# MLP up products by Strassen's scheme: seven block products instead of eight

## The chip, the cores and the metric

The kernel runs on one core of a Trainium2 chip. The metric is the device time of one execution in microseconds (us); the kernel before has a median of 1849.1 us over three runs (1847.06 to 1849.63).

## What is computed

Three layers of width D = 1024 on S = 512 tokens: gated linear attention with an MLP, stick-breaking attention with an MLP, and a third layer of mLSTM and latent attention with an MLP. All of it is float32. The change touches the first product of each MLP:

```
def sq_relu_mlp(x, w_up, w_down):
    h = jax.nn.relu(x @ w_up)          # (512 x 1024) @ (1024 x 4096)
    return (h * h) @ w_down            # (512 x 4096) @ (4096 x 1024)
```

The three first products read mlp_w_up of the two layers (up0, up1) and w_ff1 of the third (ff1).

## The kernel before

Every float32 matrix product is made of three products in float32r: each operand is split into a high part (a cast on ScalarE, ACT) and a low part (the difference, on VectorE, DVE), and mm3 (lines 214 to 218) issues high x high, high x low and low x high into one PSUM bank. Activations lie with features on the partitions: H and L hold the high and low parts of the layer's input, 8 blocks of 128 features by 512 tokens.

Weights come as tiles of 1024 features by 256 columns. A list in run (lines 1481 to 1498) gives the order of all tiles. W takes the next one; _dma (line 156) brings a tile in two raw halves through SyncE's queue, with three raw buffers; _split (line 168) casts and subtracts them into wh and wl, whole tiles of which two (pool wp), or four where the pools wx are open, exist at a time.

An MLP goes in four quarters of 1024 hidden features: four up tiles (up0, up1 or ff1), then four down tiles. mk_up and mk_down in mlp_jobs build the jobs. An up tile gives two blocks of 128 hidden features. For each, proj_fm (line 223) runs over 8 feature blocks, 3 matmuls each, all 512 tokens at once, in one bank of the pool psm (three banks). ACT then takes Relu into rl, its square as high part ah, the square again, and DVE the low part al (lines 489 to 494). A down tile multiplies the eight blocks A of the quarter and DVE adds the result to Z (lines 275, 506).

The first up quarter, the last down quarter and, in the first two MLPs, the last tile of the last up quarter are cut at token 256 (A_ and B_, 256 columns a matmul), since they overlap with the norms at the edges of the MLP (boundary). What lies between is here called the middle. It has 11 whole up tiles in quarters 1 to 3 of each of the first two MLPs and 12 in the third. A scheduler sets the order of the engines in the middle; at the edges PE's order is written by hand.

Of the kernel before, what the change touches and what calls it, by code (L numbers as in the profile page):

```python
# [10 lines left out]
F32 = mybir.dt.float32  # L11
# [7 lines left out]
P = 128  # L19
# [35 lines left out]
LAG = 2  # L55
MLA_FIRST = "1040603131"
MLA_FILL = ["101201010201011", "011101210111101", "000022010111122", "111100000113001"]
ML_FILL = "201401111116"
ML_LAST = 8


class Job:
# [5 lines left out]
    def weights(self):  # L68
        if self.w is None:
            self.w = self.model.W(*self.key)  # L70
        return self.w
# [9 lines left out]
class Model:  # L81
# [15 lines left out]
    def setup(self):  # L97
        nc, ctx, I = self.nc, self.ctx, self.I
        self.cp = cp = self.pool(ctx, "const", 1)
        self.rawp = self.pool(ctx, "rawp", 3)  # L100
        self.wp = self.pool(ctx, "wp", 2)
        self.wx = [None] * 2
# [47 lines left out]
    def stream(self, order, wide, eased):  # L150

        self.order, self.wide, self.eased = order, wide, eased
        self.raws, self.ws, self.done = {}, {}, {}
        self.pos = 0
# [12 lines left out]

    def _split(self, i, n=4):

        if i >= len(self.order) or i < self.pos:  # L170
            return
        nc = self.nc
        if i not in self.ws:
            self._dma(i)
            pool = self.wp
            for p0, p1 in self.wide:
                if p0 <= i < p1 and (i - p0) % 4 >= 2:
                    pool = self.wx[i % 2]
            if pool is None:
                return  # L180
            self.ws[i] = tuple(pool.tile([P, KC, 256], F32R, tag=n, name=f"{n}{i}") for n in ("wh", "wl"))
            self.done[i] = 0
        (hi, lo), w, q = self.ws[i], self.order[i][2], self.done[i]
        self.done[i] = min(4, q + n)
        while q < self.done[i]:

            e = min(self.done[i], q // 2 * 2 + 2)
            a, r = slice(q * 2, e * 2), self.raws[i][q // 2][:, q % 2 * 2:q % 2 * 2 + (e - q) * 2, :w]
# [7 lines left out]
    def ahead(self, n=1):  # L196
        for j in range(n):
            self._split(self.pos + j)
# [24 lines left out]
    def proj_fm(self, w, half, src, seg=FULL, ps=None, k0=0):  # L223
# [4 lines left out]
        for k, (h, l) in list(enumerate(src))[k0:]:  # L228
            self.mm3(ps, (w[0][:, k, a], w[1][:, k, a]), (h[:, seg], l[:, seg]), k == 0, k == n - 1)
        return ps  # L230

    def proj_tm(self, w, tb, n, ps=None):
# [3 lines left out]
        for k in range(KC):  # L236
            self.mm3(ps, (self.H[k][:, a], self.L[k][:, a]),
                     (w[0][:, k, :n], w[1][:, k, :n]), k == 0, k == KC - 1)
# [11 lines left out]
    def open_l(self):  # L250
        self.ls = ExitStack()
        self.l2, self.l3 = self.pool(self.ls, "l2", 2), self.pool(self.ls, "l3", 3)
        self.lh = self.pool(self.ls, "lh", 4)

    def open_wx(self):
        self.xs_ = ExitStack()
        self.wx = [self.pool(self.xs_, "wx", 1) for _ in range(2)]

    def close_wx(self):
        self.xs_.close()  # L260
        self.wx = [None] * 2
# [195 lines left out]
    def out_begin(self, jobs, A, n):  # L457

        for i, job in enumerate(jobs):
            ps = []  # L460
            for k in range(n):
                for hf in range(2):
# [7 lines left out]
                    self.mm3(ps[hf], (w[0][:, k, a], w[1][:, k, a]), (A[k][0][:, A_], A[k][1][:, A_]), k == 0, False)  # L470
# [3 lines left out]
    def mlp_jobs(self, up, down, acc, resid=True, final=None):  # L474
# [3 lines left out]
        for q in range(4):  # L478
            A = {}

            def mk_up(q, pr, A):
                def fn(w, seg):
                    n = seg.stop - seg.start
                    for hf in range(2):
# [4 lines left out]
                        r = self.l2.tile([P, S], F32, tag="rl", name=self.nm("rl"))[:, :n]  # L489
# [6 lines left out]
                return Job(self, up, q * 4 + pr, fn)  # L496
# [30 lines left out]
    def gla(self, A, out):  # L527
# [23 lines left out]
        w = self.ws[0] = tuple(w0p.tile([P, KC, 272], F32R, name=n) for n in ("wh0", "wl0"))  # L551
        self.done[0] = 0
# [172 lines left out]
    def proj_steps(self, w, half, src, evac, seg=FULL):  # L725
# [4 lines left out]
        for k, (h, l) in enumerate(src):  # L730
            self.mm3(ps, (w()[0][:, k, a], w()[1][:, k, a]), (h[:, seg], l[:, seg]), k == 0, k == KC - 1)
# [5 lines left out]
    def tm_steps(self, w, tb, n, evac):  # L737
        ps = self.acc_tile()[:, :n]
        a = slice(tb * P, tb * P + P)
        for k in range(KC):  # L740
            self.mm3(ps, (self.H[k][:, a], self.L[k][:, a]), (w()[0][:, k, :n], w()[1][:, k, :n]),
                     k == 0, k == KC - 1)
# [694 lines left out]
    def out2_steps(self, w, i, ms, A):  # L1437

        ps = [self.acc_tile() for _ in ms]
        for k in range(4):  # L1440
            for m, p in zip(ms, ps):
                while A[4 + k] is None:
                    yield
                wv = [x.rearrange("p (a b) c -> p a (b c)", b=2)[:, k, m * P:m * P + P] for x in w()]
                self.mm3(p, wv, A[4 + k], k == 0, k == 3)
# [3 lines left out]
                yield  # L1449

    def out2_begin(self, out, A):

        w = out.weights()
        for m in range(3):
            ps = self.acc_tile()[:, :256]
            self.begun[m] = ps
            for k in range(3):
                wv = [x.rearrange("p (a b) c -> p a (b c)", b=2)[:, k, m * P:m * P + P] for x in w]
                self.mm3(ps, wv, (A[k][0][:, A_], A[k][1][:, A_]), k == 0, False)
                yield  # L1460

    def out2_jobs(self, A):
# [3 lines left out]
        def mk(i):  # L1466
            def fn(w, seg):
                wv = [x.rearrange("p (a b) c -> p a (b c)", b=2) for x in w]
                for m in range(4):
                    c = i * 4 + m  # L1470
                    ps = self.begun.pop(c, None)
                    ps = self.proj_fm(wv, m, A[:4], seg, ps, 0 if ps is None else 3)
# [6 lines left out]
    def run(self):  # L1479
# [3 lines left out]
        order, wide = n4("gla_v"), []  # L1483
        for hp in range(2):
            order += [("gla_q", hp, 256), ("gla_k", hp, 256), ("gla_g", hp * 2, 256), ("gla_g", hp * 2 + 1, 256)]
        p = len(order)
        order += n4("gla_o") + mlp("up0", "down0") + n4("sb_v")
        wide.append((p, len(order)))
        order += [("sb_qk", i, 256) for i in range(8)]
        p = len(order)  # L1490
        order += n4("sb_o") + mlp("up1", "down1")
        order += [("w2_q", 0, 256), ("w2_k", 0, 256), ("w2_cq", 0, 256), ("w2_ck", 0, 208)]
        wide.append((p, len(order)))
        order += [("w2_v", 0, 256), ("w2_o", 0, 256), ("w2_v", 1, 256), ("w2_o", 1, 256)]
        order += [("w2_out", 2, 256), ("w2_out", 3, 256)]
        p = len(order)
        order += [("w2_out", 0, 256), ("w2_out", 1, 256)] + mlp("ff1", "ff2")
        wide.append((p, len(order)))
        at = lambda n, i: next(j for j, o in enumerate(order) if o[:2] == (n, i))

# [3 lines left out]
        self.stream(order, wide, eased)  # L1504
# [3 lines left out]
        for l in range(2):  # L1508
# [8 lines left out]
            self.open_wx()  # L1517
            self.open_l()
# [5 lines left out]
            for q in range(4):  # L1524
                if q:
                    self.run_jobs(mlp[q][0][:3])
                    for seg in (A_, B_) if q == 3 else (FULL,):
                        mlp[q][0][3](seg)
                if q < 3:
                    self.run_jobs(mlp[q][1])  # L1530
# [8 lines left out]
            self.ls.close()  # L1539
            self.close_wx()  # L1540
# [4 lines left out]
        self.open_wx()  # L1545
        self.open_l()
# [8 lines left out]
        for q in range(4):  # L1555
            if q:
                self.run_jobs(mlp[q][0])
            self.run_jobs(mlp[q][1][:3])
            for seg in (A_, B_) if q == 3 else (FULL,):
                mlp[q][1][3](seg)  # L1560
        self.ls.close()
        self.close_wx()
        self.zs.close()

# [89 lines left out]
```

## Time and profile before

| | |
|---|---|
| median of three runs | 1849.1 us |
| profiled execution | 1848.37 us, span 1846.6 us |
| PE (TensorE matmul) busy | 1795.9 us, 97%, 10592 instructions |
| DVE busy | 953.2 us, 52% |
| ACT busy | 869.5 us, 47% |
| GpSimd (POOL) busy | 270.2 us, 15% |
| HBM | 152.68 MB read, 85 GB/s over the span |

The span runs from the first to the last instruction of the profiled execution. Matmuls are pipelined: a matmul's own duration in the trace is longer than the distance to the next one's start, so the cost of a matmul is read as the length of an unbroken stretch divided by the matmuls in it. Durations on the other engines are those of one instruction; in a row of them, starts lie a little closer.

### The profile page before, as it was taken

The numbers are of one execution on the slowest core, as the hardware profiler recorded it, in microseconds if no ns is written. First come the engines' busy times: TensorE is split into PE (matmuls) and PEld (weight loads), VectorE is DVE, ScalarE is ACT, GpSimd is POOL, SyncE is SP. The second block draws the span as 40 slices with busy tenths as digits, with TensorE's granted clock in tenths as the row PEclk, the third lists the DMA queues.
The fourth block names the chain that finished last, engine by engine and source line by source line (L and its number), as shares of the span: only waits on it lengthen the run. The fifth ranks groups of instructions, "written<-read, shape, count | busy, mean of one in ns | idle before, by whom it ended". The sixth has DMA issues, their size and how long they took to land. (4 is left out here: it accounts for less than half of the span.)

```text
span 1846.6 us, 26425 instructions
## 1 busy us (share of the span) xinstructions
PE 1795.9 (97%) x10592; PEld 1572.5 (85%) x10592; DVE 953.2 (52%) x1438; ACT 869.5 (47%) x1726; POOL 270.2 (15%) x315
## 2 busy tenths in 40 slices
PE   8999989999999999988999999989999999999999
PEld 8899988888889978878988888989897898888887
DVE  4545673333336378878533333374897764333331
ACT  5445462424153478854624242346778563424240
POOL 1002240000012233342200000144002220000000
PEclk9999999999999999989999999999999999999999
DMA  5212323232332212113223333232113223332221
GB/s 184 92 46 79 106 87 120 91 92 91 98 99 69 78 46 60 56 58 103 92 92 91 97 100 100 69 110 84 38 38 101 69 68 121 101 99 92 92 80 46
DMA packets 47610, 158.58 MB, mean 86 GB/s; under 512 B 5168, under 2 KB 8896, under 8 KB 47488
## 3 DMA queue, kind: packets, MB, share of 16 engines
q1 hardware_dynamic: 44752, 150.88, 26.2%
q0 software_dynamic: 1296, 3.92, 0.7%
q8 instruction: 83, 1.36, 0.3%
q10 hardware_dynamic: 1440, 2.10, 0.3%
q14 instruction: 39, 0.32, 0.1%
HBM read 152.68 MB, written 4.19 MB: 85 GB/s over the span
## 5 line engine op out<-in xcount | busy, mean ns | idle before, releaser
L189 ACT CAST wh<-raw 128x1024 fp32r<-128x1024 f32 (+1 forms) x306 | 290.9, 974 | 507.9 <-PE mm L217 443.7
L216 PE MATMUL mm<-ah,wh 128*128 128x512 f32 (+1 forms) x1264 | 436.6, 345 | 6.8 <-ACT ah L891 3.5
L216 PE MATMUL mm<-H,wh 128*128 128x512 f32 (+1 forms) x1248 | 441.4, 354 | 0.1
L217 PE MATMUL mm<-L,wh 128*128 128x512 f32 (+1 forms) x1248 | 432.6, 347 | 6.1 <-DVE L L330 6.0
L217 PE MATMUL mm<-al,wh 128*128 128x512 f32 (+1 forms) x1264 | 432.7, 342 | 1.7 <-DVE al L524 1.5
L218 PE MATMUL mm<-H,wl 128*128 128x512 f32 (+1 forms) x1248 | 432.8, 347 | 0.0
L218 PE MATMUL mm<-ah,wl 128*128 128x512 f32 (+1 forms) x1264 | 431.4, 341 | 0.0
L191 DVE TENSOR_TENSOR wl<-raw,wh 128x1024 fp32r<-128x1024 f32 (+1 forms) x260 | 296.1, 1154 | 201.4 <-ACT wh L189 199.8
L216 PEld LDWEIGHTS mm<-ah,wh 128*128 128x128 f32 x1264 | 240.4, 190 | 37.8 <-ACT ah L891 3.7
L217 PEld LDWEIGHTS mm<-al,wh 128*128 128x128 f32 x1264 | 240.6, 190 | 31.8 <-DVE al L524 2.2
L218 PEld LDWEIGHTS mm<-ah,wl 128*128 128x128 f32 x1264 | 240.6, 190 | 29.0
L217 PEld LDWEIGHTS mm<-L,wh 128*128 128x128 f32 x1248 | 235.5, 189 | 34.8 <-DVE L L330 6.8
L218 PEld LDWEIGHTS mm<-H,wl 128*128 128x128 f32 x1248 | 234.9, 188 | 31.6
L216 PEld LDWEIGHTS mm<-H,wh 128*128 128x128 f32 x1248 | 235.3, 189 | 30.0 <-issue 0.8
L191 POOL TENSOR_TENSOR wl<-raw,wh 128x1024 fp32r<-128x1024 f32 (+2 forms) x46 | 109.1, 2373 | 776.5 <-ACT wh L189 736.0
L506 DVE TENSOR_TENSOR Z<-Z,mm 128x512 f32<-128x512 f32 (+1 forms) x98 | 57.5, 588 | 260.3 <-PE mm L218 260.3
L494 DVE TENSOR_TENSOR al<-rl,ah 128x512 fp32r<-128x512 f32 (+1 forms) x124 | 91.4, 744 | 161.9 <-ACT rl L493 161.9
L216 PE MATMUL mm<-wh,H 128*128 128x256 f32 (+2 forms) x568 | 163.3, 288 | 7.0 <-ACT wh L189 7.0
L218 PE MATMUL mm<-wh,L 128*128 128x256 f32 (+2 forms) x568 | 160.4, 282 | 0.0
L217 PE MATMUL mm<-wl,H 128*128 128x256 f32 (+2 forms) x568 | 160.1, 282 | 0.0
L216 PEld LDWEIGHTS mm<-wh,H 128*128 128x128 f32 x568 | 107.6, 190 | 8.7 <-ACT wh L189 7.7
L490 ACT ACTIVATE rl<-mm 128x512 f32<-128x512 f32 (+1 forms) x124 | 61.6, 497 | 107.7 <-PE mm L218 103.7
(328 smaller groups left out, 2085.2 us busy)
## 6 DMA issues: line engine op xcount, KB each, us to landing
raw<-in_up SPq DMA_DIRECT2D x64, 512.0 KB, 4.3
raw<-in_down SPq DMA_DIRECT2D x64, 512.0 KB, 4.2
raw<-in_ff SPq DMA_DIRECT2D x64, 512.0 KB, 4.4
raw<-in_sb_qk SPq DMA_DIRECT2D x16, 512.0 KB, 3.8
raw<-in_gla_g SPq DMA_DIRECT2D x8, 512.0 KB, 4.2
raw<-in_gla_o SPq DMA_DIRECT2D x8, 512.0 KB, 4.2
raw<-in_sb_v SPq DMA_DIRECT2D x8, 512.0 KB, 3.8
raw<-in_sb_o SPq DMA_DIRECT2D x8, 512.0 KB, 3.7
```

The costliest lines, as they stand in the source:

```text
L189: nc.scalar.copy(hi[:, a, :w], r)
L191: eng.tensor_tensor(lo[:, a, :w], r, hi[:, a, :w].bitcast(F32), op=ALU.subtract)
L216: mm(ps, l[0], r[0], start=start, stop=False)
L217: mm(ps, l[0], r[1], start=False, stop=False)
L218: mm(ps, l[1], r[0], start=False, stop=stop)
L490: nc.scalar.activation(r, ps, AF.Relu)
L494: nc.vector.tensor_tensor(l, r, h.bitcast(F32), op=ALU.subtract)
L506: nc.vector.tensor_tensor(self.Z[:, c, seg], self.Z[:, c, seg], ps, op=ALU.add)
```

## The change

Of the 1024 features, the 256 columns and the 512 tokens of an up tile each is cut in two, which makes a 2 x 2 by 2 x 2 block product with blocks of 512 features by 128 columns and 512 features by 256 tokens. Winograd's form of Strassen's scheme makes it of seven block products instead of eight. A block product is 4 feature blocks x 3 matmuls of 256 columns (product).

- From the weight tile, _combine makes on DVE four sums S1 to S4 (of 128 x 512 each), and high and low parts of A11, of the pairs S1 S3 and S2 S4, and of A12 A22: three half tiles of 1024 and one piece of 512. Before, a tile had two halves of 1024.
- From H and L (or Z, where it holds their sum), mid_operands makes the operands T1 to T4 once an MLP, in parts ahead of the jobs of the first down quarter.
- fast_up issues the products. Bank a takes A11 B11, then on top of it S2 T2, S1 T1 and S4 B22; ACT copies it to the tile C between. Bank d takes S3 T3, then A22 T4; bank b takes A12 B21. DVE adds d and b to parts of C, ACT applies Relu and squares, DVE makes the low part. Two of a tile's products (third, fourth) are issued among those of the next tile.
- Weights lie in half tiles (class Weights, half_tile): four of them always, eight at the edges, six in the middle; raw halves have four buffers instead of three. Pools are closed and opened between edge and middle (open_edge, open_mid).
- In the middle PE's order is now that of the program (middle).

```diff
+    def half_tile(self, i, g):
+        pool = self.wp if i in self.home else min(self.slots, key=lambda p: self.slots[p][0])
+        name = f"{i}_{g}"
+        self.seq += 1
+        self.slots[pool] = self.slots[pool][1:] + [self.seq]
+        return tuple(pool.tile([P, 4, 256], F32R, tag=n, name=f"{n}{name}") for n in ("wh", "wl"))
...
+    def _combine(self, i):
+        nc, tt, w = self.nc, self.nc.vector.tensor_tensor, self.ws[i]
+        r0, r1 = self.raws[i]
+        one, two = slice(0, P), slice(P, 256)
+
+        def parts(pair, t, *names):
+            nc.scalar.copy(pair[0], t)
+            tt(pair[1], t, pair[0].bitcast(F32), op=ALU.subtract)
+            for n, a in zip(names, (one, two)):
+                w[n] = [x[:, :, a] for x in pair]
+
+        w["A11"] = tuple(self.vp.tile([P, 4, P], F32R, tag=n, name=f"{n}{i}") for n in ("vh", "vl"))
+        parts(w["A11"], r0[:, :, one])
+        s13, s24 = (self.sp.tile([P, 4, 256], F32, tag="S", name=self.nm("S")) for _ in range(2))
+        tt(s13[:, :, one], r0[:, :, two], r1[:, :, two], op=ALU.add)
+        tt(s13[:, :, two], r0[:, :, one], r0[:, :, two], op=ALU.subtract)
+        parts(self.half_tile(i, 0), s13, "S1", "S3")
+        yield
+        tt(s24[:, :, one], s13[:, :, one], r0[:, :, one], op=ALU.subtract)
+        tt(s24[:, :, two], r1[:, :, one], s24[:, :, one], op=ALU.subtract)
+        parts(self.half_tile(i, 1), s24, "S2", "S4")
+        yield
+        parts(self.half_tile(i, 2), r1, "A12", "A22")
+        self.raws.pop(i)
...
+    def open_mid(self):
+        self.es = ExitStack()
+        self.more_units(self.es, 6 - UNITS)
+        self.vp, self.sp = self.pool(self.es, "vp", 1), self.pool(self.es, "sp", 2)
+        self.tp, self.rp = self.pool(self.es, "tp", 1), self.pool(self.es, "rp", 2)
...
+    def mid_operands(self, z):
...
+        def less(n, k, seg, t):
+            o = self.sp.tile([P, 4, 256], F32, tag="S", name=self.nm("T"))
...
+            tt(o, a[0], t, op=ALU.subtract)
+            for x in a[1:]:
+                tt(o, o, x, op=ALU.add)
+            X[n] = tuple(self.tp.tile([P, 4, 256], F32R, tag=n + e, name=self.nm(n + e)) for e in "hl")
+            nc.scalar.copy(X[n][0], o)
+            tt(X[n][1], o, X[n][0].bitcast(F32), op=ALU.subtract)
+            return o
...
+        less("T3", 1, B_, block(0, B_))
+        t1 = less("T1", 0, B_, block(0, A_))
+        yield
+        t2 = less("T2", 1, B_, t1)
+        yield
+        less("T4", 1, A_, t2)
+
+    def product(self, ps, w, x, start):
+        n = 0
+        for k in range(4):
+            for i, j in ((0, 0), (0, 1), (1, 0)):
+                self.nc.tensor.matmul(ps, w[i][:, k], x[j][:, k], start=start and n == 0, stop=n == 11,
+                                      skip_group_check=not start)
+                n += 1
+
+    def fast_up(self, jobs):
...
+        def hidden(C, m, A):
+            act(A[0], C[:, m], AF.Square)
+            act(C[:, m], C[:, m], AF.Square)
+            tt(A[1], C[:, m], A[0].bitcast(F32), op=ALU.subtract)
+
+        def third(J):
+            w, a, d, C, A = J
+            self.product(a, w["S4"], self.X["B22"], False)
+            act(C[:, 0, B_], a, AF.Relu)
+            act(C[:, 0, A_], C[:, 0, A_], AF.Relu)
+            hidden(C, 0, A[0])
+
+        def fourth(J):
+            w, a, d, C, A = J
+            self.product(d, w["A22"], self.X["T4"], False)
+            tt(C[:, 1, A_], C[:, 1, A_], d, op=ALU.add)
+            act(C[:, 1], C[:, 1], AF.Relu)
+            hidden(C, 1, A[1])
+
+        X = self.X
+        for job in jobs:
+            w = job.weights(ahead=False)
+            a, d = bank("a"), bank("d")
+            C = self.rp.tile([P, 2, S], F32, tag="C", name=self.nm("C"))
+            self.ahead(1, 2)
+            self.product(a, w["A11"], X["B11"], True)
+            act(C[:, 0, A_], a, AF.Copy)
+            if prev:
+                third(prev)
+            else:
+                self.product(d, w["S3"], X["T3"], True)
+            self.ahead(1, 2)
+            self.product(a, w["S2"], X["T2"], False)
+            act(C[:, 1, A_], a, AF.Copy)
+            if prev:
+                fourth(prev)
+            else:
+                b = self.fast_second(w)
+            self.ahead(1, 2)
+            self.product(a, w["S1"], X["T1"], False)
+            act(C[:, 1, B_], a, AF.Copy)
+            if prev:
+                self.product(d, w["S3"], X["T3"], True)
+                b = self.fast_second(w)
+            tt(C[:, 1, B_], C[:, 1, B_], d, op=ALU.add)
+            tt(C[:, 0, A_], C[:, 0, A_], b, op=ALU.add)
+            prev = w, a, d, C, job.hidden()
+        third(prev)
+        fourth(prev)
...
+        fast = {at(n, i) for n in ("up0", "up1", "ff1") for i in range(4, 16 if n == "ff1" else 15)}
...
+    def middle(self, mlp, z, halves):
+        self.open_mid()
+        with self.tc.manual_schedule(engines={mybir.EngineType.PE}):
+            parts = self.mid_operands(z)
+            for q in range(4):
+                if q:
+                    n = 4 - halves * (q == 3)
+                    self.fast_up(mlp[q][0][:n])
...
```

The order on PE, at the start of quarter 1 of the first MLP. Before, the first matmuls of the second half of its first tile (mm is the bank, H and L the input, wh and wl the weights):

```order
L216 MATMUL mm_3310<-H,wh_3204 128x512
L217 MATMUL mm_3310<-L,wh_3204 128x512
L218 MATMUL mm_3310<-H,wl_3205 128x512
L216 MATMUL mm_3310<-H,wh_3204 128x512
L217 MATMUL mm_3310<-L,wh_3204 128x512
```

Now the second tile there, with the first matmul of each product, twelve of which follow each other (a_3378, d_3379 are the banks of the tile before, a_3477, d_3478 and mm_3587 its own, b):

```order
L369 MATMUL a_3477<-H,vh_3381 128x256
...
L369 MATMUL a_3378<-H,wh_1_3310 128x256
...
L369 MATMUL a_3477<-T2h_3158,wh_1_3420 128x256
...
L369 MATMUL d_3379<-T4h_3228,wh_2_3314 128x256
...
L369 MATMUL a_3477<-T1h_3088,wh_0_3389 128x256
...
L369 MATMUL d_3478<-T3h_3082,wh_0_3389 128x256
...
L369 MATMUL mm_3587<-H,wh_2_3450 128x256
```

Each pair of products into a_3477 has one other product between; S4 of the tile before comes between the first two, A22 between the next.

The order on ACT in the same run of four tiles. Before, evacuation of the first blocks (rl, ah) and the casts of the next tile (wh):

```order
L490 ACTIVATE rl_3303<-mm_3278 128x512
L492 ACTIVATE ah_3276<-rl_3303 128x512
L493 ACTIVATE rl_3303<-rl_3303 128x512
L189 CAST wh_3488<-raw_0_3420 128x1024
L490 ACTIVATE rl_3335<-mm_3310 128x512
L189 CAST wh_3488<-raw_1_3422 128x1024
L492 ACTIVATE ah_3308<-rl_3335 128x512
L493 ACTIVATE rl_3335<-rl_3335 128x512
```

Now, from the first copies of the first tile (L409, L416, L423 copy bank a after A11, S2 and S1):

```order
L409 ACTIVATE C_3380<-a_3378 128x256
L416 ACTIVATE C_3380<-a_3378 128x256
L392 ACTIVATE C_3380<-C_3380 128x256
L236 CAST wh_0_3488<-S_3484 128x1024
L423 ACTIVATE C_3380<-a_3378 128x256
L236 CAST vh_3480<-raw_0_3374 128x512
L409 ACTIVATE C_3479<-a_3477 128x256
L236 CAST wh_1_3524<-S_3485 128x1024
L391 ACTIVATE C_3380<-a_3378 128x256
L384 ACTIVATE ah_3469<-C_3380 128x512
L416 ACTIVATE C_3479<-a_3477 128x256
L385 ACTIVATE C_3380<-C_3380 128x512
```

A cast of 1024 stands ahead of the first tile's S1 copy (L423); the cast of A11's piece (vh) ahead of the second tile's first copy; a cast, a Relu (L391) and a square (L384) ahead of its second (L416).

The order on DVE, from the last sums into Z of the down quarter before this run (L450) to the first add into C (L428) of the run:

```order
L450 SCALAR_TENSOR_TENSOR Z_1955<-Z_1955,mm_3270 128x512
L237 TENSOR_TENSOR wl_0_3390<-S_3385,wh_0_3389 128x1024
L245 TENSOR_TENSOR S_3484<-raw_0_3374 128x4x128
L244 TENSOR_TENSOR S_3484<-raw_0_3374,raw_1_3376 128x4x128
L450 SCALAR_TENSOR_TENSOR Z_1955<-Z_1955,mm_3322 128x512
L237 TENSOR_TENSOR wl_1_3421<-S_3386,wh_1_3420 128x1024
L248 TENSOR_TENSOR S_3485<-S_3484,raw_0_3374 128x4x128
L450 SCALAR_TENSOR_TENSOR Z_1955<-Z_1955,mm_3348 128x512
L249 TENSOR_TENSOR S_3485<-raw_1_3376,S_3485 128x4x128
L237 TENSOR_TENSOR wl_2_3451<-raw_1_3320,wh_2_3450 128x1024
L237 TENSOR_TENSOR vl_3382<-raw_0_3318,vh_3381 128x512
L428 TENSOR_TENSOR C_3380<-C_3380,mm_3437 128x256
```

The parts of the second tile (raw_1_3320 and its sums S_3385, S_3386) and the sums of the third (S_3484, S_3485) now stand on DVE before the run's first add; before, DVE had only low parts of whole tiles between the sums into Z.

## Rows read from the trace of the kernel before

**Rows 1.** The page: instructions, busy time and share of the span, PE's clock.
```profile
span 1846.6 us, 26425 instructions
...
PE 1795.9 (97%) x10592; PEld 1572.5 (85%) x10592; DVE 953.2 (52%) x1438; ACT 869.5 (47%) x1726; POOL 270.2 (15%) x315
...
PE   8999989999999999988999999989999999999999
...
PEclk9999999999999999989999999999999999999999
```

**Rows 2.** Busy time by stretch: up quarters 1 to 3 of three MLPs, nine stretches.
```profile
core 0: us, PE busy (x) PEld busy (x) DVE busy (x) ACT busy (x) POOL busy (x), PEclk, DMA share, GB/s
325.03:369.81 44.78, 44.78 (x193) 36.19 (x192) 15.16 (x16) 20.40 (x30) 0.00 (x0) 1.00 0.31 94
...
503.25:536.43 33.18, 33.18 (x145) 27.05 (x144) 11.33 (x11) 14.89 (x22) 2.40 (x1) 1.00 0.29 95
...
1576.34:1620.73 44.39, 44.39 (x194) 36.08 (x193) 15.15 (x16) 20.41 (x30) 0.00 (x0) 1.00 0.30 95
...
sum 377.45, PE 377.45 PEld 306.65 DVE 128.82 ACT 172.65 POOL 4.82; mean PE 41.94 PEld 34.07 DVE 14.31 ACT 19.18 POOL 0.54
```

**Rows 3.** Busy time by stretch: matmuls of 256 columns, last of 208.
```profile
536.43:547.32 10.89, 10.89 (x97) 10.88 (x96) 4.21 (x5) 7.18 (x14) 2.40 (x1) 1.00 0.30 96
547.32:572.85 25.53, 25.53 (x219) 25.53 (x218) 8.96 (x14) 3.01 (x5) 2.40 (x1) 1.00 0.14 43
1168.53:1179.84 11.31, 11.31 (x97) 11.31 (x96) 4.21 (x5) 7.17 (x14) 2.40 (x1) 1.00 0.30 94
1254.25:1259.60 5.35, 5.35 (x51) 5.35 (x49) 3.43 (x6) 5.35 (x14) 5.35 (x8) 1.00 0.01 3
```

**Rows 4.** ACT's instructions by line and form: busy us, mean ns, idle before.
```profile
L189 ACT CAST wh<-raw 128x1024 fp32r<-128x1024 f32 x252 | 258.1, 1047 | 498.6 <-PE mm L217 436.7 <-issue 31.0 <-POOL wl L191 10.1
...
L492 ACT ACTIVATE ah<-rl 128x512 fp32r<-128x512 f32 x68 | 43.0, 632 | 1.1
...
L189 ACT CAST wh<-raw 128x512 fp32r<-128x512 f32 x52 | 31.1, 624 | 9.3 <-PE mm L217 7.0 <-DMA raw<-in_gla_v 1.8
...
L490 ACT ACTIVATE rl<-mm 128x256 f32<-128x256 f32 x56 | 21.1, 378 | 21.1 <-PE mm L218 17.1 <-DVE al L494 4.0
```

**Rows 5.** DVE's instructions by line and form.
```profile
L191 DVE TENSOR_TENSOR wl<-raw,wh 128x1024 fp32r<-128x1024 f32 x211 | 259.3, 1244 | 194.9 <-ACT wh L189 193.5 <-issue 0.4
...
L506 DVE TENSOR_TENSOR Z<-Z,mm 128x512 f32<-128x512 f32 x62 | 42.7, 688 | 221.5 <-PE mm L218 221.5
...
L191 DVE TENSOR_TENSOR wl<-raw,wh 128x512 fp32r<-128x512 f32 x48 | 35.8, 761 | 6.5 <-ACT wh L189 6.3
...
L506 DVE TENSOR_TENSOR Z<-Z,mm 128x256 f32<-128x256 f32 x36 | 14.8, 416 | 38.8 <-PE mm L218 38.8
```

**Rows 6.** DVE's timeline (start, us) in a down quarter: two in a row.
```profile
382.03 2.36 DVE L191 TENSOR_TENSOR wl<-raw,wh 128x1024 fp32r<-128x1024 f32 x2 [0.16 <-ACT wh L189]
```

**Rows 7.** Busy time by stretch: down quarter 1 of the first MLP.
```profile
369.81:414.33 44.52, 44.52 (x194) 36.06 (x192) 15.02 (x16) 9.65 (x12) 0.00 (x0) 1.00 0.32 95
```

**Rows 8.** The page, DMA issues: count, KB each, us to landing.
```profile
raw<-in_up SPq DMA_DIRECT2D x64, 512.0 KB, 4.3
```

**Rows 9.** PE's timeline in an up quarter: first matmul of the next half.
```profile
330.62 0.40 PE L216 MATMUL mm<-H,wh 128*128 128x512 f32 x1
```

**Rows 10.** ACT's timeline there: the evacuation of the half before.
```profile
330.82 0.60 ACT L490 ACTIVATE rl<-mm 128x512 f32<-128x512 f32 x1 [3.83 <-PE mm L218]
```

**Rows 11.** Timeline of all engines, 653 to 654 us: PE waits for ACT.
```profile
653.23 0.58 ACT L812 CAST K<-mm 64x512 fp32r<-64x512 f32 x1
...
653.86 0.49 PE L841 MATMUL z<-K,Q 128*128 128x512 f32 x1 [0.35 <-ACT K L812]
```

More of the change, by code (lines that the diff above doesn't have):

```diff
@@ L55 @@
 LAG = 2
+UNITS = 4
 MLA_FIRST = "1040603131"
@@ L59, with __init__, at @@
 ML_LAST = 8
+class Weights:
+    def __init__(self, parts, nk):
+        self.parts, self.nk = parts, nk
+    def at(self, k, cols):
+        return tuple(x[:, k % self.nk, cols] for x in self.parts[k // self.nk])
 class Job:
@@ L166, in _dma, with more_units @@
             self.raws[i].append(r)
-    def _split(self, i, n=4):
-        if i >= len(self.order) or i < self.pos:
+    def more_units(self, es, n):
+        pool = self.pool(es, "wx", n)
+        self.slots[pool] = [0] * n
+        es.callback(lambda: self.slots.pop(pool))
+    def half_tile(self, i, g):
[4 more added lines that the diff above has]
+        return tuple(pool.tile([P, 4, 256], F32R, tag=n, name=f"{n}{name}") for n in ("wh", "wl"))
+    def _split(self, i, n=4):
+        if i >= len(self.order) or i < self.pos or i in self.later and len(self.slots) == 1:
+            return
+        if i in self.fast:
+            if i not in self.ws:
+                self._dma(i)
+                self.ws[i], self.done[i] = {}, self._combine(i)
+            for _ in range(1 if n < 4 else 3):
+                next(self.done[i], None)
             return
@@ L174, in _split @@
             self._dma(i)
[L175 to L183, printed above, removed]
+            self.ws[i], self.done[i] = Weights([], 4), 0
+        parts, w, q = self.ws[i].parts, self.order[i][2], self.done[i]
         self.done[i] = min(4, q + n)
         while q < self.done[i]:
-            e = min(self.done[i], q // 2 * 2 + 2)
-            a, r = slice(q * 2, e * 2), self.raws[i][q // 2][:, q % 2 * 2:q % 2 * 2 + (e - q) * 2, :w]
+            g = q // 2
+            if g == len(parts):
+                parts.append(self.half_tile(i, g))
+            hi, lo = parts[g]
+            e = min(self.done[i], g * 2 + 2)
+            a = slice(q % 2 * 2, q % 2 * 2 + (e - q) * 2)
+            r = self.raws[i][g][:, a, :w]
             nc.scalar.copy(hi[:, a, :w], r)
@@ L263, in z_from_h, with fast_second @@
+    def fast_second(self, w):
+        b = self.acc_tile()[:, :256]
+        self.product(b, w["A12"], self.X["B21"], True)
+        return b
     def z_from_h(self):
@@ L1503, in run @@
             (("down1", 13), ("w2_ck", 0)), (("w2_out", 0), ("ff1", 3)))]
-        self.stream(order, wide, eased)
+        later = {at(n, i) for n in ("gla_o", "sb_o") for i in (2, 3)}
+        self.stream(order, fast, home, later, eased)
         self.setup()
@@ L1523, in run @@
             self.z_from_h()
[L1524 to L1530, printed above, removed]
+            self.es.close()
+            self.middle(mlp, self.Z, 1)
+            self.open_edge()
             acc2.update({0: self.new_acc(), 256: self.new_acc()})
@@ L1554, in run @@
         self.boundary(out, norm, mlp[0][0])
[L1555 to L1562, printed above, removed]
-        self.zs.close()
+        self.es.close()
+        self.middle(mlp, None, 0)
+        self.run_jobs(mlp[3][1][:3])
+        for seg in (A_, B_):
+            mlp[3][1][3](seg)
+        self.es.close()
+        self.zs.close()
+    def middle(self, mlp, z, halves):
[6 more added lines that the diff above has]
+                    self.fast_up(mlp[q][0][:n])
+                    for job in mlp[q][0][n:]:
+                        job(A_)
+                        job(B_)
+                if q < 3:
+                    for job in mlp[q][1]:
+                        next(parts, None)
+                        job()
+        if z is not None:
+            self.es.close()
 def _tiles(w, cols=None):
```

117 lines of the change are left out of this document (67 added, 50 removed).

## The prediction

> **What bounds the kernel now.** I read the page's totals first: TensorE (PE) is busy 1795.9 of 1846.6 us, at the full granted clock (2.4 GHz) in all slices but one [rows 1]. The profiled execution took 1848.37 us, of which 1.8 lie outside the span; the median of the three runs is 1849.1, so 0.7 us are added at the end. Then I cut the timeline into stretches. Nine of them are exactly the work that the change rewrites: the whole up tiles of quarters 1 to 3 in three MLPs, 11 + 11 + 12 = 34 tiles. Together they last 377.45 us, with PE busy in every microsecond, VectorE (DVE) in 128.82, ScalarE (ACT) in 172.65 [rows 2]. Four tiles take 44.4 us and 192 matmuls, 231 ns each; one tile costs 377.45 / 34 = 11.10 us. PE alone sets their length, so what PE saves there is saved, as long as the other engines keep up.
>
> **What goes and what comes on PE.** A tile had 2 halves x 8 feature blocks x 3 = 48 matmuls of 512 columns. It gets 7 products x 4 x 3 = 84 of 256: 21504 columns instead of 24576, an eighth less. The order has 11481 PE rows instead of 10257; 1224 = 34 x 36, so all 34 tiles are changed and PE's matmuls elsewhere stay in number. The price of a 256-column matmul stands in stretches that were cut at token 256. The last up tile of the first MLP: 10.89 us / 96 = 113.4 ns; the same tile in the second: 11.31 / 96 = 117.8; a down stretch whose moving operand is the separate tiles ah, al: 25.53 / 216 = 118.2 [rows 3]. So this matmul costs about half of a 512-column one (115.7), and hardly more: that is what makes the scheme worth anything. It cannot get much shorter, as 208 columns still take 5.35 / 48 = 111.5 ns [rows 3].
>
> Of the seven products, three stream H and L (mean of the two up rows, 115.6), four stream new T tiles, laid out apart like ah, al (118.2): (3 x 115.6 + 4 x 118.2) / 7 = 117.1. A tile then takes 84 x 117.1 = 9.84 us, a product of 12 matmuls 1.40 us. Saved: 377.45 - 34 x 9.84 = 42.9 us. Bounds by the rows: all at 113.4, 53.6 us; all at 118.2, 39.9 us.
>
> A rule is weighed here. The Trainium skill (TensorE: Matmul & The Clock Gate, Back-to-back issue gap) gives a warm gap of N / 2.4 + 2.5 ns, that is 109.2 and 215.8 ns; by it the saving would be 34 x (48 x 0.2158 - 84 x 0.1092) = 40.3 us. The trace disagrees with both figures (113.4 to 118.2, and 231), so rows are used.
>
> **The other engines.** ACT, a tile: three casts of 1024 (1.05), one of 512 (0.62), three copies out of PSUM and two Relu of 256 (0.38), one Relu and four squares of 512 (0.63) [rows 4]: 3.15 + 0.62 + 1.90 + 3.15 = 8.8 us, against 20.4 / 4 = 5.1 before [rows 2]. DVE: three low parts of 1024 (1.18 in a row, 1.24 alone), one of 512 (0.76), four sums of 512 and two low parts of the hidden tile (0.69), three adds from PSUM (0.42) [rows 5, 6]: 3.54 + 0.76 + 4.14 + 1.26 = 9.7 us, before 15.2 / 4 = 3.8. Beside a PE tile of 9.84 both are nearly full: 89% and 99%. The cover is the down quarter: DVE works 15.0 and ACT 9.7 of its 44.5 us [rows 7], and by the order the whole first tile and most of the second are combined there. In the run of four tiles (39 us) DVE then has, by the rows between the first add into C and the last, some 11 of 1024, 10 of 512 and 12 of 256: 13.0 + 6.9 + 5.0 = 25 us. So I cost DVE at nothing. If that cover went, DVE would set the tile.
>
> The operands T1 to T4 are made once an MLP, beside the first down quarter: four subtractions and four low parts, 8 x 1.24 = 9.9 us of DVE (in the third MLP, where H and L are first added again, six more, 17.4), in the 29 us that DVE is free there; nothing on the path, since PE can fill two more banks before it waits for a sum into Z. The DMAs are the same 64 for each up matrix, 4.3 us from issue to landing [rows 8], 1 MB each 9.84 us; SP's order is unchanged but for two swaps around x_mid. Two more raw halves are buffered. The edges of each MLP and the attention stages keep their PE work, and I cost their reordered casts at nothing: PE's own matmuls cover them as before.
>
> **The new waits.** Before, each output had a bank of its own. Now one bank, a, carries A11B11, then S2T2, S1T1, S4B22 on top, and ACT must copy it out before the next product may be added. From the end of PE's group to the copy's start takes 0.20 us (next group's first matmul at 330.62, ACT at 330.82) [rows 9, 10], the copy 0.38, and PE starts 0.05 after ACT ends (653.23 + 0.58 = 653.81, PE 653.86) [rows 11]: 0.63 us, under one product put between, 1.40. So 0.77 us of other ACT work is hidden. What is queued ahead decides, and ACT works in order. Ahead of the A11 copy stands at most the small cast: 0.63 + 0.62 = 1.25 us, hidden. Ahead of the S2 copy stand, from S4's end, a cast, a Relu and a square: 0.20 + 1.05 + 0.38 + 0.63 + 0.38 + 0.05 = 2.69 us, in two products, 2.81: hidden by 0.1. In the first tile of a run the S1 copy has one product only, and a cast ahead: 1.68 - 1.40 = 0.28 us lost, nine times, 2.5 us. For the thin margins I take 0.1 us in each other tile, 2.5. Where a run ends, the last add, Relu, two squares and the subtraction (0.42 + 0.63 + 1.26 + 0.69, hops 0.5, one cast) make 4.6 us; the down tile needs that operand after 21 matmuls, 4.9 us. Together 5 us; bounds nothing, and 19 us where both copies of each tile miss by 0.28 (34 x 0.56). The chain up to the sum: 42.9 - 5 = 37.9; 1848.4 - 37.9 = 1810.5 for the profiled execution, with 0.7 **1811 us**.
>
> **Rivals.** (a) *ACT is late.* Casts ahead of the copies wait in their turn for DVE, and PE stands behind them at two products of each tile, 0.3 to 0.7 us a tile beyond the 5 us: 1821 to 1835. For: ACT at 89%, a margin of 0.1. Against: in the stretch at 1254 ACT was busy in all of it, and PE waited for nothing [rows 3].
> (b) *Slower: DVE sets the tile.* Its queue stands in order, and four of its low parts each wait for an ACT cast (0.9 on average). If nothing is made ahead, a tile is 9.7 + 3.6 = 13.3 us on DVE, more than the 11.1 of before. It decides from 42.9 / 34 = 1.26 us of wait a tile; half of the excess over PE, 1.7 + hops of 0.3, gives 68 - 43 = +25 us, 1874. Against: only four tiles follow each other, with 29 us of free DVE before them.
> (c) *The saving is eaten up:* 1.15 to 1.37 us a tile lost, 1845 to 1853, by the same waits; nothing in the rows singles it out. That the change does less than it says is excluded by the count of rows.
>
> **The numbers.** Forecast 0.76 (1796, all rows at 113.4 and no wait, to 1822), (a) 0.13, (b) 0.08, (c) 0.03. A measurement tells 0.2%, 3.7 us, from nothing. Faster 0.76 + 0.13 = 0.89, same 0.03, slower 0.08. The range reaches from 1797 to 1832: the bound of rates and waits together is 39.9 - 19 = 20.9 us, 1828, and a little of (a).
>
> **To see.** The nine stretches at 84 matmuls a tile, 113 to 118 ns each and about 39.5 us for four; PE idle in front of L369 of about 5 us, put down to ACT's copies; DVE under 30 of 39 us in a run. Wrong if the matmuls of L369 come 125 ns apart or more, or PE waits over 0.5 us a tile, or an edge moves by over 3 us.

## The result and the profile after

The changed kernel takes **1825.1 us** (median of four runs, 1823.18 to 1826.51) against 1849.19 of the kernel before beside it (1847.06 to 1849.63): a ratio of 0.9871, 95% interval 0.9854 to 0.9888. It is faster by 24 us; 38 were forecast. The profiled execution took 1826.51 us, its span is 1824.6 us.

The page of the changed kernel, totals and PE's slices [rows 1]:

```profile
span 1824.6 us, 29591 instructions
...
PE 1765.2 (97%) x11816; PEld 1606.5 (88%) x11816; DVE 1175.0 (64%) x1774; ACT 973.8 (53%) x1942; POOL 276.5 (15%) x315
...
PE   8999999999999999989999999988999999999999
...
PEclk9999999999999999999999999999999999999999
```

PE is busy 30.7 us less, but the span is only 22.0 us shorter: some work was shortened, and some idle time came in. To find which, the span is cut at the same places as before. First the nine stretches of whole up tiles, which the change rewrites (busy time by stretch, columns as in [rows 2]):

```profile
326.14:365.88 39.74, 39.74 (x337) 39.56 (x336) 26.70 (x38) 28.57 (x50) 0.00 (x0) 1.00 0.39 123
...
494.55:524.40 29.85, 29.85 (x254) 29.70 (x252) 17.91 (x25) 20.47 (x36) 0.00 (x0) 1.00 0.40 129
...
1568.29:1608.08 39.79, 39.79 (x337) 39.61 (x336) 26.71 (x38) 28.57 (x50) 0.00 (x0) 1.00 0.38 123
...
sum 337.53, PE 337.53 PEld 336.02 DVE 222.77 ACT 240.76 POOL 0.00; mean PE 37.50 PEld 37.34 DVE 24.75 ACT 26.75 POOL 0.00
```

They sum to 337.53 us against 377.45 [rows 2]: 39.9 us saved, more than the 38 that were forecast, all of them from these stretches. The rest of the span is cut at the starts and ends of the down quarters that lie beside them (from PE's timeline; profiled executions; "first" are the three down quarters of quarter 0, "other downs" those of quarters 1 and 2; each is a sum):

| stretch, us | before | after | difference |
|---|---|---|---|
| start to the first down quarter | 280.35 | 280.29 | -0.1 |
| first down quarters | 133.71 | 136.35 | +2.6 |
| other downs | 267.22 | 267.30 | +0.1 |
| nine up stretches | 377.45 | 337.53 | -39.9 |
| edges and attention between first and second MLP | 376.45 | 379.06 | +2.6 |
| edges and attention between second and third MLP | 363.37 | 375.99 | +12.6 |
| last down quarter to the end | 48.05 | 48.08 | 0.0 |

Almost 18 us are lost outside the rewritten tiles: 2.6 in the first down quarters and 15.2 in the edges and attention stages, most of them in the part with mLSTM and latent attention. PE's waits after (engine, line and what it waited for; us in total, times, longest us):

```profile
PE st L473 <- DVE fold L462: 9.5, 6, 4.7
...
PE qp L1391 <- DMA wuq<-in_w_uq: 6.1, 1, 6.1
...
PE mm L276 <- DVE al L669: 2.1, 2, 1.1
```

The wait for wuq, a weight of the latent attention, did not exist before. PE's timeline of the changed kernel around it (start us, us, instruction, in brackets the idle time before it and what ended it):

```profile
1264.19 0.28 PE L277 MATMUL mm<-wh,L 128*128 128x256 f32 x1
1270.54 1.62 PE L1391 MATMUL qp<-wuq,cT 128*128 128x192 f32 x4 [6.07 <-DMA wuq<-in_w_uq]
1271.95 1.06 PE L1392 MATMUL kv<-wuk,cT 128*128 128x256 f32 x2
```

and of the kernel before at the same instruction:

```profile
1286.71 0.28 PE L218 MATMUL mm<-wh,L 128*128 128x256 f32 x1
1286.83 0.82 PE L1210 MATMUL qp<-wuq,cT 128*128 128x192 f32 x4
1287.49 0.59 PE L1211 MATMUL kv<-wuk,cT 128*128 128x256 f32 x2
```

Before, the matmuls follow without a gap. Now PE stands still for 6 us, and then the same group of matmuls takes 1.62 us instead of 0.82, at a granted clock of 0.50 (1270.54 to 1272.80). Why the load is late stands on GpSimd's timeline, after:

```profile
1262.21 1.28 POOL L224 TENSOR_TENSOR wl<-raw,wh 128x512 fp32r<-128x512 f32 x1 [7.77 <-PE pa L1287]
1264.10 1.27 POOL L224 TENSOR_TENSOR wl<-raw,wh 128x512 fp32r<-128x512 f32 x1 [0.62 <-ACT wh L222]
1265.31 0.61 POOL L142 DMA_DIRECT2D wuq<-in_w_uq  x1
```

and before:

```profile
1274.30 2.61 POOL L191 TENSOR_TENSOR wl<-raw,wh 128x512 fp32r<-128x512 f32 x2 [2.82 <-ACT wh L189]
...
1283.88 0.61 POOL L130 DMA_DIRECT2D wuq<-in_w_uq  x1 [2.96 <-PE mm L218]
```

The load of wuq is issued by GpSimd, in order. Before, two low parts of the weight tile w2_o0 were done 7 us ahead of it, and it went out 2.95 us before PE needed it, in time. Now these low parts are held back by PE and ACT until 1262, and the load goes out 1.0 us after PE is ready for it. It is also slower: 5.1 us from issue to landing, where this load took 2.8 before. The loads of two raw halves were issued beside it (from 1262.04 on); whether they slow it was not tried.

### The profile page after: what moved, and what is told of

It is laid out like the page before. It is cut to its first block, busy times and chain, and to the rows that moved or that the text cites. A ratio compares the mean times of both kernels' runs of the same rounds, so it can differ in the third digit from the quotient of the medians.

```text
span 1824.6 us, 29591 instructions
## 1 busy us (share of the span) xinstructions
PE 1765.2 (97%) x11816; PEld 1606.5 (88%) x11816; DVE 1175.0 (64%) x1774; ACT 973.8 (53%) x1942; POOL 276.5 (15%) x315
## 5 line engine op out<-in xcount | busy, mean ns | idle before, releaser
L224 DVE TENSOR_TENSOR wl<-raw,wh 128x1024 fp32r<-128x1024 f32 (+1 forms) x192 | 221.2, 1157 | 88.5 <-ACT wh L222 85.8
L222 ACT CAST wh<-raw 128x1024 fp32r<-128x1024 f32 (+2 forms) x238 | 223.1, 951 | 101.7 <-PE mm L276 65.0
L275 PE MATMUL mm<-H,wh 128*128 128x256 f32 (+1 forms) x704 | 228.9, 325 | 0.2 <-ACT sl L1198 0.2
L276 PE MATMUL mm<-L,wh 128*128 128x256 f32 (+1 forms) x704 | 219.8, 312 | 4.5 <-DVE L L505 4.5
L277 PE MATMUL mm<-H,wl 128*128 128x256 f32 (+1 forms) x704 | 219.6, 312 | 0.0
L236 ACT CAST wh<-S 128x1024 fp32r<-128x1024 f32 x68 | 71.3, 1048 | 166.6 <-PE mm L276 152.0
L276 PEld LDWEIGHTS mm<-L,wh 128*128 128x128 f32 x704 | 134.9, 192 | 8.8 <-DVE L L505 5.3
L277 PEld LDWEIGHTS mm<-H,wl 128*128 128x128 f32 x704 | 134.2, 191 | 8.2
L275 PEld LDWEIGHTS mm<-H,wh 128*128 128x128 f32 x704 | 134.7, 191 | 6.6 <-issue 0.8
L237 DVE TENSOR_TENSOR wl<-S,wh 128x1024 fp32r<-128x1024 f32 x68 | 83.2, 1223 | 74.8 <-ACT wh L236 74.8
```

The costliest lines, as they stand in the source:

```text
L236: nc.scalar.copy(pair[0], t)
L237: tt(pair[1], t, pair[0].bitcast(F32), op=ALU.subtract)
L275: mm(ps, l[0], r[0], start=start, stop=False)
L276: mm(ps, l[0], r[1], start=False, stop=False)
L277: mm(ps, l[1], r[0], start=False, stop=stop)
```

## The experiments

After the result there were two explanations. **Theory A**: the change alters which buffer a weight tile gets. Half tiles go in turn to the pool whose slot was used longest ago, wp or wx. By the program's order, w2_k lies in wx after the change, and w2_ck, the last tile that PE reads there, in the two wp halves that w2_o0 gets next; GpSimd must wait for PE's last read, and wuq stands behind it on GpSimd's queue. Before, w2_o0 got the place of w2_k, free long before. **Rival B**: the program has a smaller scratch for the DMAs that GpSimd issues (8192 bytes, a setting that the change also makes), which delays them.

**e1_home** pins one more tile of each of two MLPs to wp, so that the turn of the halves afterwards falls as it did before:

```diff
         home = {at(*x) for n in ("down0", "down1", "ff2") for x in ((n, 0), (n, 12))}
+        home |= {at(n, 13) for n in ("down0", "down1")}
```

> Only change against the changed kernel: the second down tile of the last down quarter of the first two MLPs is also put into the four always open weight halves, so that the weights of w2_k, and not those of w2_ck, lie where w2_o comes next (and sb_v 1, not sb_v 3, where the second sb_qk tile comes). Theory A (the 18 us lost outside the nine stretches come mostly from this rotation: GpSimd holds a low part of w2_o back until the last matmul on w2_ck, and the loads of wuq stand behind it on GpSimd's queue): the 6.1 us wait of PE for wuq goes, and the half-clock microseconds behind it, 8 to 12 us less, 1813 to 1817 us. Rival B (the loads are late for another reason, the smaller descriptor scratch or the DMA itself): within 2 us of 1825.

Measured: **1814.33 us** (1813.11 to 1815.07), ratio to before 0.9808 (0.9791 to 0.9824), 10.8 us less than the changed kernel. GpSimd's timeline:

```profile
1257.68 0.60 POOL L142 DMA_DIRECT2D wuq<-in_w_uq  x1 [0.88 <-PE mm L277]
```

and PE's, in e1_home:

```profile
1260.62 0.28 PE L277 MATMUL mm<-wh,L 128*128 128x256 f32 x1
1260.74 0.81 PE L1391 MATMUL qp<-wuq,cT 128*128 128x192 f32 x4
```

The load goes out 3.06 us ahead of its use, lands 2.7 us after its issue, and no wait is left. The stretch between second and third MLP falls from 375.99 to 366.51 us, that between first and second by 1.6. Theory A stands.

**e2_nofast** keeps the new pools, half tiles and PE's order in the middle, but makes the up tiles as before (48 matmuls of 512 columns) and no T operands:

```diff
-        fast = {at(n, i) for n in ("up0", "up1", "ff1") for i in range(4, 16 if n == "ff1" else 15)}
+        fast = set()
...
-            parts = self.mid_operands(z)
+            parts = iter(())
...
-                    self.fast_up(mlp[q][0][:n])
+                    self.run_jobs(mlp[q][0][:n])
```

> The changed kernel with its half tiles, pools, four raw halves and PE's hand order in the middle, but no seven-product tile: all up tiles as eight products, and no T operands. Theory A (the nine stretches gave their 40 us, and the new weight rotation costs 15 to 18 us elsewhere whatever the up product is): 1849 + 13 to 17 = 1862 to 1866. Rival C (the loss outside comes from the work of the seven products, its casts and low parts on ScalarE and VectorE): 1847 to 1852.

Measured: **1861.66 us** (1860.57 to 1862.41), ratio 1.0065 (1.005 to 1.008). The loss is there without a single product of the new scheme: the stretch between second and third MLP is 375.43 us, +12.1 against before, and the same wait stands in PE's timeline:

```profile
1293.16 1.62 PE L1391 MATMUL qp<-wuq,cT 128*128 128x192 f32 x4 [5.99 <-DMA wuq<-in_w_uq]
```

The nine up stretches sum to 377.02 us, as before. So nearly all of the 12.6 us comes without the new products, and e1_home, which only pins two more tiles, gives back 9.5 of it. The first down quarters are +1.0 us and the stretch between first and second MLP +1.4, where the changed kernel has +2.6 each; the operands T are a part of the rest at most.

**e3_scratch** gives the kernel before the smaller scratch:

```diff
-    nc = bacc.Bacc("TRN2", target_bir_lowering=False, num_devices=1)
+    nc = bacc.Bacc("TRN2", target_bir_lowering=False, num_devices=1, dynamic_dma_scratch_size=8192)
```

> The kernel before, with the descriptor scratch of 8192 that the changed kernel has. Theory A: same as before, 1849 +- 2. Rival B (GpSimd's loads of wuq and wuk, or others, wait for room in the smaller scratch): wuq lands later than its 3.0 us median and the time grows by 5 us or more.

Measured: **1849.52 us**, ratio 1.0003 (0.9994 to 1.0013). The smaller scratch costs the kernel before nothing, and e1_home has it too and no wait for wuq; Rival B falls.

**e4_nocover** measures what the order of products is worth. In each tile after a run's first, A11, S2 and S1 follow each other on bank a with nothing between:

```diff
             act(C[:, 0, A_], a, AF.Copy)
-            if prev:
-                third(prev)
-            else:
+            if not prev:
...
             act(C[:, 1, B_], a, AF.Copy)
             if prev:
+                third(prev)
+                fourth(prev)
```

> The changed kernel, but in every tile after the first of a run the products into one bank follow each other (A11, S2, S1), and the two products of the tile before (S4, A22) come behind them, not between. The prediction's round trip is 0.63 us bare (0.20 to the copy, 0.38, 0.05): with no product between, PE should stand twice a tile for it, 25 tiles x 2 x 0.63 = 31 us, so 1856. If the copies also wait for casts ahead of them on ScalarE, 1.0 or more each, 1870 and above. If a copy costs PE nothing even without cover, 1825.

Measured: **1903.24 us** (1902.37 to 1905.47), ratio 1.0292 (1.0276 to 1.0307), 78 us over the changed kernel: of the three forecasts, 1870 and above. PE's waits:

```profile
PE a L369 <- ACT C L409: 41.8, 25, 2.2
PE a L369 <- ACT C L414: 11.8, 25, 0.5
```

and the first two of the nine stretches (busy time by stretch; the clock is the third column from the end):

```profile
325.54:373.21 47.67, 41.13 (x337) 39.93 (x336) 25.90 (x38) 28.24 (x50) 0.00 (x0) 1.00 0.29 98
418.31:468.53 50.22, 43.69 (x338) 42.30 (x337) 25.92 (x38) 28.26 (x50) 0.00 (x0) 0.93 0.28 93
```

The copy after S2 (L414) costs 0.47 us of wait. The view counts a wait from the end of the matmul before; from start to start PE loses 0.75 - 0.12 = 0.63 us there (at 350.31), just the bare round trip that the prediction used. The copy after A11 (L409) costs 1.67 us on average. It stands on ACT behind what is left of the tile before, and then waits for DVE as well. ACT's timeline for one of them:

```profile
346.76 0.41 ACT L392 ACTIVATE C<-C 128x256 f32<-128x256 f32 x1
347.70 0.38 ACT L409 ACTIVATE C<-a 128x256 f32<-128x256 f32 x1 [0.53 <-DVE al L386]
```

ACT stands idle for 0.53 us until DVE's low part al (line 386) is done. Tiles C have two buffers (pool rp), and al is the last that reads the one which this copy writes. So the 1.67 us are not the price of the missing products alone: the run delays the end of the tile before as well.

The waits are 53.6 of the 78.4 us by which the nine stretches grew (to 415.88). The other 24.7 come behind the waits, and only about half of them go with the clock. The two stretches shown have the same six waits, 6.5 us each. At a clock of 1.00 the first grew by 7.9 us, 1.4 more than its waits: the first two matmuls behind each wait come late. At 0.93 the second grew by 10.6, 4.1 more than its waits. Three of the nine stretches kept 1.00; in the changed kernel all nine have it.

**e5_raw3** is e1_home with three raw buffers instead of four (rival D: the fourth raw half is what keeps the parts of the next tile ahead):

```diff
-        self.rawp = self.pool(ctx, "rawp", 4)
+        self.rawp = self.pool(ctx, "rawp", 3)
```

> The kernel of e1_home (1814.3 us) with three raw halves instead of four. Theory A2 (of the 5 us still lost outside the middle, some 4 come from the fourth raw half: it lets casts and low parts of coming tiles start earlier, and the scheduler puts them on VectorE ahead of short steps that PE waits for, as the 1.2 us low part ahead of the softmax reciprocal at 1366): the edges and the latent attention give 2 to 4 us back, and where the seven-product tiles still find their raw halves in time, 1810 to 1812. Rival D (the middle needs the fourth: a combined tile holds both raw halves until its third step, so the next load starts late): PE waits for a weight in L369, 5 us or more, 1819 and above.

Measured: **1836.51 us** (1831.58 to 1841.44), ratio 0.9932 (0.9918 to 0.9946), 22 us over e1_home. The profiled execution is the fastest of the six, 17 us over that of e1_home. PE's waits in it:

```profile
PE mm L276 <- DVE al L669: 7.4, 3, 2.8
...
PE a L369 <- ACT C L423: 5.8, 9, 1.1
```

and the sum of the nine stretches:

```profile
sum 343.82, PE 337.98 PEld 336.16 DVE 233.92 ACT 239.00 POOL 0.00; mean PE 37.55 PEld 37.35 DVE 25.99 ACT 26.56 POOL 0.00
```

The middle loses 6.1 us against e1_home (337.72), at nine places by the wait for the copy in line 423; the first down quarters lose 9.3 (145.68 against 136.37 in e1_home). Theory A2 falls. Rival D has the direction, but PE waits for no weight in L369: the waits are for the copy and for al. The buffer is needed, and more for the first parts beside the down quarter than for the run itself.

**e6_ease** is e1_home with the low parts of the first two down tiles of an MLP on DVE instead of GpSimd:

```diff
-        eased = [(at(*a), at(*b) + 3) for a, b in (
+        eased = [(at(*a), at(*b) + (1 if b[1] == 3 and b[0] != "sb_v" else 3)) for a, b in (
```

> The kernel of e1_home with the low parts of the first two down tiles of each MLP on VectorE instead of GpSimd. Theory A3 (the first down quarters of the first two MLPs last 45.9 us instead of 44.6 because a low part al of 256 columns took 2.61 us beside GpSimd's low part, and 0.43 without it): that wait of 1.1 to 1.4 us goes twice, 1811.5 to 1812.5. Rival (VectorE is full there with the T operands, 2.4 us in front of al, and gets two more low parts): the wait stays or grows, 1814 to 1817.

It asks after the 2.6 us of the first down quarters. In the changed kernel DVE does there:

```profile
280.56 2.36 DVE L342 TENSOR_TENSOR T<-Z 128x1024 f32<-128x1024 f32 x2 [1.16 <-PE mm L277]
282.84 1.22 DVE L224 TENSOR_TENSOR wl<-raw,wh 128x1024 fp32r<-128x1024 f32 x1
283.97 2.61 DVE L669 TENSOR_TENSOR al<-rl,ah 128x256 fp32r<-128x256 f32 x1
```

beside this on GpSimd,

```profile
283.15 3.16 POOL L224 TENSOR_TENSOR wl<-raw,wh 128x1024 fp32r<-128x1024 f32 x1 [14.67 <-ACT wh L222]
```

and PE waits for al:

```profile
286.64 0.50 PE L276 MATMUL mm<-al,wh 128*128 128x512 f32 x1 [1.05 <-DVE al L669]
```

In e6_ease DVE's timeline has there

```profile
284.70 0.42 DVE L669 TENSOR_TENSOR al<-rl,ah 128x256 fp32r<-128x256 f32 x1
285.04 1.22 DVE L224 TENSOR_TENSOR wl<-raw,wh 128x1024 fp32r<-128x1024 f32 x1
```

The same subtraction takes 0.42 us when GpSimd is idle and 2.61 when GpSimd runs its own; the three first down quarters are 133.57 us, as before. But the kernel measured **1813.74 us** (1812.1 to 1814.39), ratio 0.981 (0.9797 to 0.9823): not to be told from e1_home. Against it the first down quarters gained 2.8 us, while the start took 1.65 more and the stretch between second and third MLP 1.3 more. The wait was real, but its removal does not show in the total. Why is not shown: e8_all has the same edit, its first down quarters take 133.57 us too, and its other two stretches take 280.06 and 366.67 us, 1.0 and 1.2 less than here. So what ate the gain may be no more than what one execution differs from the next.

**e7_first** is e1_home with one product more between in a run's second tile (S3 T3 before S4 B22), to cover the 0.25 us that PE waits there:

```diff
             act(C[:, 0, A_], a, AF.Copy)
+            if n == 1:
+                self.product(d, w["S3"], X["T3"], True)
             if prev:
                 third(prev)
...
-            if prev:
+            if n > 1:
                 self.product(d, w["S3"], X["T3"], True)
```

> The kernel of e1_home, but in the second tile of each run the product S3 T3 comes ahead of S4 B22 of the first tile, so that ScalarE's copy of the first tile's third sum has two products of cover like the others. By the prediction's working that copy misses by 0.28 us a run; the trace shows PE 0.25 us late at that place in all nine runs, and nowhere else in the runs. So 2.2 us less, 1812; if the wait only moves to the next copy, 1814.

Measured: **1816.3 us** (1814.38 to 1819.68), ratio 0.9827 (0.9814 to 0.984); no gain, but 2 us more than e1_home. Stretches, two runs of four tiles and one of three:

```profile
326.02:366.05 40.03, 39.87 (x338) 39.66 (x336) 26.79 (x38) 28.38 (x50) 0.00 (x0) 1.00 0.38 122
410.55:450.50 39.95, 39.64 (x338) 39.44 (x336) 26.78 (x38) 28.30 (x50) 0.00 (x0) 1.00 0.38 122
495.03:524.66 29.63, 29.63 (x254) 29.63 (x252) 17.82 (x25) 20.37 (x36) 0.00 (x0) 1.00 0.41 131
```

The runs of three tiles gained their 0.22 us (29.85 to 29.63). The runs of four lost 0.2 to 0.4, at the third tile, where the copy after A11 is now late:

```profile
346.15 0.39 PE L369 MATMUL a<-T2h,wh 128*128 128x256 f32 x1 [0.16 <-ACT C L409]
```

ACT's timeline there:

```profile
345.71 0.38 ACT L409 ACTIVATE C<-a 128x256 f32<-128x256 f32 x1 [0.60 <-DVE al L386]
```

As in e4_nocover, the copy stands idle for DVE's low part al, here of the first tile, whose buffer C the third one takes. Delaying S4 by a product delayed what follows it on ACT and DVE, up to that low part. A third buffer for C, which might take this wait away, was not tried.

**e8_all** joins e6_ease and e7_first. 

> e6_ease and e7_first together. If both hold, the gains add: 1809 to 1811. If only e7's, 1812.

Measured: **1814.05 us** (1812.86 to 1815.19), ratio 0.9812 (0.9799 to 0.9825). Neither forecast held. Against e7_first it is 2.25 us less, which could be the gain of e6_ease, but the runs of e7_first spread over 5.3 us. Nothing is gained over e1_home, which with its one line is the version that beats both kernels: 10.8 us under the changed kernel, 34.4 under the one before.

## Why the prediction was right, and where it was not

The direction and the mechanism of the saving hold. The forecast of 1811 us was 14 us too low: the rewritten tiles saved 2 us more than forecast, and 18 us were lost where the prediction had put nothing. That the time lies in the stated range is in part luck. It lies outside the forecast's own 1796 to 1822 and among the times of rival (a), 1821 to 1835, but ACT's copies, for which the range had been widened, cost next to nothing.

- **The price of a matmul**: 117.1 ns forecast. The nine stretches without the nine late starts give (337.53 - 9 x 0.25) / 2856 = 117.4. By operand, from the starts within the products in PE's timeline: 114.1 to 116.9 ns for H and L (115.6 forecast), 118.6 to 118.9 for T1 to T4 (118.2). So the saving in the rewritten tiles came as worked out. The figure of 109.2 ns from the Trainium skill (TensorE: Matmul & The Clock Gate, Back-to-back issue gap), weighed there, does not show in the trace; its section gives it for a single matmul by itself, and here each comes in a stream, with a weight load of its own.
- **The new waits**: 0.28 us at the S1 copy of a run's first tile, nine times. Found: 0.21 to 0.25, nine times, at the S4 that comes next on that bank. It shows in the starts, as in this place of PE's timeline after, where two of them are 0.26 and 0.22 us behind the one before instead of 0.12:

```profile
334.48 0.28 PE L369 MATMUL a<-H,vl 128*128 128x256 f32 x1
334.74 0.38 PE L369 MATMUL a<-H,wh 128*128 128x256 f32 x1
334.96 0.28 PE L369 MATMUL a<-L,wh 128*128 128x256 f32 x1
```

  The allowance of 0.1 us in each of the 25 other tiles was not needed: none of them waits. e4_nocover shows that the products between hide the copies: without them the copy after S2 costs its whole round trip. Its other wait, after A11, holds the wait for a buffer C too.
- **DVE and ACT**: DVE 25 us of 39 forecast in a run of four, 26.7 of 39.7 found; the parts are made ahead beside the down quarter, as the order showed. None of the waits of rivals (a), (b) and (c) came. e5_raw3 shows what the cover hangs on: the fourth raw half.
- **The T operands, costed at nothing**: two of the first down quarters are 1.2 and 1.3 us longer than before, where DVE's small low part came to stand beside a GpSimd subtraction. In e2_nofast, without T operands, the same two meet, DVE and GpSimd:

```profile
283.00 2.42 DVE L669 TENSOR_TENSOR al<-rl,ah 128x256 fp32r<-128x256 f32 x1 [0.34 <-ACT rl L668]
282.73 2.41 POOL L224 TENSOR_TENSOR wl<-raw,wh 128x1024 fp32r<-128x1024 f32 x1 [14.24 <-ACT wh L222]
```

  There PE waits 0.33 us instead of 1.05, and the two quarters are 0.41 and 0.55 longer than before. So the T operands account for at most 0.8 us in each; the meeting itself comes without them.
- **The step that failed**: "the edges of each MLP and the attention stages keep their PE work, and I cost their reordered casts at nothing: PE's own matmuls cover them as before". 15.2 us were lost there (18 with the first down quarters). The rows used for it told that PE was busy, not by how much each load came in time. wuq came with 0.2 us to spare before: issued at 1283.88, landed 2.75 us later, used at 1286.83. The prediction looked at the order within the middle, not at which buffer each weight gets behind it. e1_home shows that 10.8 us of the whole loss hang on the turn of the buffers, and e2_nofast that the late load comes without the seven products. The prediction's own test, an edge that moves by over 3 us, pointed there.
- **Left open**: in e1_home the first down quarters (+2.7), the stretch between first and second MLP (+1.0) and the one between second and third (+3.1) are still longer than before. For the second, DVE's timeline after shows one more case of a low part beside GpSimd's (in e1_home it is still there), beside two that run from 582.74 to 588.64, ahead of the norm's fold:

```profile
583.64 2.76 DVE L224 TENSOR_TENSOR wl<-raw,wh 128x1024 fp32r<-128x1024 f32 x1 [0.26 <-ACT wh L222]
...
589.22 0.42 DVE L462 TENSOR_TENSOR fold<-acc 128x256 f32<-128x256 f32 x1
```

  No run took this one away by itself.

## What to carry to other kernels

Where PE is the bound, fewer columns pay nearly in full (an eighth fewer gave 10.6% of the nine stretches), as long as each bank's copy has enough other products between and the operands are made ahead; both can be counted from rows before. A change of tile sizes also changes which buffer every later tile gets: follow the rotation to the next loads with little slack, above all those that an engine issues behind its own arithmetic. And test storage and order without the new arithmetic: here they cost 12 us by themselves.

## What the runs showed of the hardware

- **PE's clock after a short wait.** In the changed kernel PE waits 2.21 us for the fold, before 0.31; in these two lines, after and before:

```profile
589.70 1.22 PE L473 MATMUL st<-fold,onesd 128*128 128x256 f32 x2 [2.21 <-DVE fold L462]
600.43 0.70 PE L298 MATMUL st<-fold,onesd 128*128 128x256 f32 x2 [0.31 <-DVE fold L287]
```

  After the long wait PE's matmuls of 256 columns came 0.21 us apart instead of 0.12. Busy time by stretch in the changed kernel, from that wait's end and after it (clock third from the end):

```profile
589.70:593.02 3.32, 3.32 (x13) 3.14 (x14) 2.67 (x6) 1.28 (x3) 0.00 (x0) 0.51 0.61 204
593.14:594.50 1.36, 1.36 (x14) 1.36 (x13) 0.90 (x2) 0.37 (x1) 0.00 (x0) 1.00 0.00 0
```

  That is the lower level, 1.2 GHz, and then the upper, 2.4 GHz. Before, the instructions of the first of these stretches took 1.84 us instead of 3.32. So this wait cost 1.5 us more behind it. Not every wait of that length does: in e7_first PE waits 1.91 us at the same place, and the clock behind it stays at 1.00,

```profile
589.90:593.20 3.30, 3.30 (x27) 3.25 (x28) 3.17 (x7) 1.77 (x3) 0.00 (x0) 1.00 0.56 178
```

  and in e4_nocover a wait of 2.21 us at 348.14 left it at 1.00, while one of 2.15 at 440.96 was followed by a stretch at 0.65 (440.96 to 444.30). The waits of 0.16 to 0.31 us in the stretches of e7_first left the clock at 1.00.
- **DVE beside GpSimd.** A DVE subtraction that started at 283.97, while GpSimd's ran from 283.15 to 286.31, ended at 286.58: 2.61 us instead of 0.42. The Trainium skill (SBUF — State Buffer, SBUF: two separate sides) says that a DVE operation with two SBUF inputs and a GpSimd operation that reads SBUF take one pair of ports in turn, and that whichever starts first keeps it to its end. The trace agrees: DVE's end lies 0.27 us behind GpSimd's. In e5_raw3 the same happened to a low part of 1024 elements, 3.40 us instead of 1.22, beside GpSimd's from 286.17 to 288.59.
